# Sample's GLA products across the column groups, its state loaded earlier, more side steps in the fox gates

## The chip, the cores and the metric

One NeuronCore of a Trainium2 chip runs the whole program. The metric is the device time of one execution in microseconds, as the median of several runs. The engines are TensorE (PE, with its weight loads PEld), VectorE (DVE), ScalarE (ACT), GpSimd (POOL) and SyncE (SP, which issues most DMAs here). Each works through its own queue in order.

## The reference, cut to what matters

One layer of a hybrid decoder, in float32, for a prompt of 512 tokens and for 8 sample sequences with one new token each and 4096 cached positions in pages. Two branches run in parallel: forgetting attention (fox, 8 heads of 64) and gated linear attention (GLA, 4 heads, keys of 64, values of 128). Sigmoid gates merge them, then come an output projection and an MLP. For a sample token the GLA branch computes:

```python
b = jnp.cumsum(la, axis=1)                                   # one token: b = la
inter = jnp.einsum('blhd,bhde->blhe', qf * jnp.exp(b), S0)   # S0: (8, 4, 64, 128) state
intra = (q . k) * v                                          # with one token
S_new = exp(b)[..., None] * S0 + k (outer) v                 # returned as gla_state_sample
y = rmsnorm(inter + intra, gain) * silu(og)
```

## The kernel before, in words

Weights stream in 256 columns at a time through SP (tag raw), are split into a high part (wh, by ACT, L221) and a low part (wl, by DVE, L222), and are multiplied in three products per tile (pmm in PSUM, three buffers, two halves of 256 and 264 columns for the prompt with the samples). The main line is a list of such dense stages: fox q, k, v; gla_qk; gla_vo for values (vg) and output gates (sg); gate_f(0..3), the fox gates, each with two tanh tiles (tanh2, L1002 on, into uu) and two tiles of the fox output product; then gate_g and mix for the GLA side; then w_o and the MLP.

Two other lines of work are interleaved with it, by generators. `run(gen, nside, ndec)` advances after each dense tile the side generators by nside steps (`beside`) and the decode by an amount that follows the estimated PE time (`pump`). The decode reads the pages of keys and values of the samples (kk, kv; POOL issues these DMAs), multiplies keys on DVE (L573, L574) and values on PE (pdv). The side list holds in turn the two halves of fox for the prompt, `gla_levels` (20 steps: two for the gates, one for the diagonal, 15 for the seven levels, two that make the decayed keys kdt, with L822 to L832), `gla_sample` (five steps) and `gla_out` (four chunks of the prompt, one step each). The side work uses the px buffers of PSUM (three).

All this is program order. The framework then orders the instructions of each engine itself, by a simulated time line and with program order as priority. Buffers of a tag are slots that it hands out: a tile that is asked for (`c8()` in the code) waits until an earlier tile of the tag has had its last use. Tag c8, 8 KB per partition, has nine slots. They hold, one after another, the inputs, q and k of fox, vtok, the fox output o (two tiles, used until gate_f's last product), qk (T1, read by the levels until L827), vg, sg, then AT and bq (T2) of the levels, uu (one for gate_f(0) and (1), one for (2) and (3)), S0 of the sample, yh and yl of gla_out, and ug of gate_g. In the trace all of these are named c.

`gla_sample` first loads its state S0 (1 MB, L922). Qm holds the decayed queries spread out so that sample b's product lands in row b of its head's 32 rows. The product po adds up eight matmuls for each of four heads: head h reads rows (h%2)*64 to +64 of Qm and S0 and writes the 32 rows from h*32 of one PSUM buffer. In float32 each matmul of the code is two instructions on PE. pvo holds q.k (L939 to L942). L945 on make y, and four steps of two samples each update S0 (km, px, L974), which L977 stores.

The lines that the change touches in the main program:

```python
    for n in range(4):
        run(gate_f(n), LP, PC)
    drain("levels", "new")
```

Of the kernel before, what the change touches and what calls it, by code (L numbers as in the profile page):

```python
# [19 lines left out]
NB = 8  # L20
H = 8
GH = 4
FF = 4096
EPS = 1e-6
TS = T + NB
FP, LP, LQ = 3, 1, 1
PA, PB, PC, PD, PE_ = 1, 1.2, 0.6, 0.6, 1
LK, LV = 0, 2
TO = 1
# [20 lines left out]
def _emit(ctx, tc, I, O):  # L50
    nc = tc.nc
# [9 lines left out]
    def new(shape, tag, dt=F32, bufs=None):  # L61
        n_[0] += 1
        return sb.tile(shape, dt, tag=tag, name=f"{tag}_{n_[0]}", bufs=bufs or BUFS[tag])

    def c8(dt=F32, shape=None):
        return new(shape or [128, 4, 512], "c8", dt)
# [5 lines left out]
    def cst(shape, name, dt=F32):  # L72
        return const.tile(shape, dt, tag=name, name=name)

    def small(shape, name, bufs=2, dt=F32):
        n_[0] += 1
        return sb.tile(shape, dt, tag=name, name=f"{name}_{n_[0]}", bufs=bufs)
# [3 lines left out]
    def mm(out, lhsT, rhs, start, stop):  # L81

        clock[0] += np.prod(rhs.shape[1:]) * (4 if rhs.dtype == F32 else 1) / (4 if out.shape[0] == 32 else 1) / 2400
        PE.matmul(out=out, lhsT=lhsT, rhs=rhs, start=start, stop=stop)  # L84
# [72 lines left out]
    for lg in (4, 3, 2, 1, 0):  # L157
        a = cst([128, 32], f"lm{lg}", I32)
        b = new([128, 32], "qb", I32)
# [97 lines left out]
    def take():  # L257
        while len(ready) < 2 and plan:
            prepare()
        return ready.pop(0)  # L260
# [282 lines left out]
    gl = {}  # L543
# [164 lines left out]
    def gla_qk(w_i):  # L708
        if not w_i:
            gl["qk"] = c8()  # L710
        T1 = gl["qk"]
        w = take()[0]
        sc_ = 1.0 if w_i else 0.125
        for m in range(2):
            p0, p1 = dense_fm2(w, m, xh, xl, 8)
            S.activation(out=T1[:, 2 * w_i + m, 0:256], in_=p0[:, 0:256], func=AF.Copy, scale=sc_)
            S.activation(out=T1[:, 2 * w_i + m, 256:512], in_=p1[:, 0:256], func=AF.Copy, scale=sc_)
            S.activation(out=sq[:, 2 * w_i + m, :], in_=p1[:, 256:264], func=AF.Copy, scale=sc_)
# [6 lines left out]

    def level(sz, hp, Gt, AT, Dg):
        for e in range(2):
# [12 lines left out]
            if sz == 64:  # L740
                S.copy(out=AT[0:64, us, 64:128], in_=p[0:64, 0:256].rearrange("p (u t) -> p u t", t=64))
                continue
            p3 = p[:, 0:128].rearrange("p (u t) -> p u t", t=32)
            if sz == 32:
                for j in (0, 64):
                    S.copy(out=AT[j:j + 32, us, j + 32:j + 64], in_=p3[j:j + 32])
            elif sz == 16:
# [4 lines left out]

    def gla_levels():
        T1 = gl["qk"]
        AT = gl["AT"] = c8(shape=[128, 16, 128])
        G.memset(AT, 0.0)
        T2 = gl["bq"] = c8()

        for hp in range(2):
            p = ps("x")  # L760
            mm(p, wau[32:48, hp * 128:(hp + 1) * 128], lr[32:48, 0:512], True, True)
            x, y, a = (new([128, 512], "ts") for _ in range(3))
# [18 lines left out]
        for hp in range(2):  # L781
            pr = new([128, 512], "ts")
            V.tensor_tensor(out=pr, in0=T1[:, hp, :], in1=T1[:, 2 + hp, :], op=ALU.mult)
            for e in range(2):
# [10 lines left out]
        for u in range(len(units) + 1):  # L795
            if u < len(units):
                sz, hp = units[u]
                Et, Gt = new([128, 512], "ts"), new([128, 512], "ts")
                v4 = lambda a: a.rearrange("p (n f s) -> p n f s", f=2, s=sz)
                b4, E4, G4, q4, k4 = v4(T2[:, hp, :]), v4(Et), v4(Gt), v4(T1[:, hp, :]), v4(T1[:, 2 + hp, :])  # L800
                nb = 512 // (2 * sz)
# [6 lines left out]
            if prev is not None:  # L808
                level(*prev, AT, Dg)
            prev = (sz, hp, Gt) if u < len(units) else None  # L810
# [3 lines left out]
        for j in range(4):  # L814
            r = slice(j * 32, j * 32 + 32)
            S.copy(out=AT[r, :, r], in_=Dg[r])

        kdt = gl["kdt"] = [T2[:, hp, :].rearrange("p (c k) -> p c k", k=128) for hp in range(2)]
        for hp in range(2):
            b_, Et, kd = T2[:, hp, :], new([128, 512], "ts"), new([128, 512], "ts")  # L820
            S.activation(out=Et, in_=b_, func=AF.Exp, scale=1.0 / 16)
            V.tensor_tensor(out=T2[:, 2 + hp, :], in0=Et, in1=T1[:, hp, :], op=ALU.mult)  # L822
            bc = b_.rearrange("p (c t) -> p c t", t=128)
# [15 lines left out]
    def vo_new(is_v, n, raws):  # L839
        e, pr = sproj(hsT, raws)  # L840
        for j in range(2):
            R = slice((2 * n + j) * 32, (2 * n + j) * 32 + 32)
            mm(pr[R, 0:128], sel, e[:, j * 128:(j + 1) * 128], True, True)
        R = slice(n * 64, n * 64 + 64)
        S.copy(out=vrow[R, 0:128] if is_v else vrow[R, 128:256], in_=pr[R, 0:128])
        if is_v:
# [71 lines left out]
    ysT = cst([128, 4, 32], "ysT")  # L918

    def gla_sample():  # L920
        S0 = c8(shape=[128, 16, 128])
        nc.sync.dma_start(out=S0, in_=I["state_gla"].rearrange("o b (a e) k v -> (o e k) (b a) v", e=2))  # L922
        eas = cst([128, 2, 8], "eas")
        S.activation(out=eas, in_=las, func=AF.Exp, scale=1.0 / 16)
        Qm = new([128, 2, 256], "ts")
        G.memset(Qm, 0.0)
        V.tensor_tensor(out=Qm[:, :, 0:256:33], in0=sq[:, 0:2, :], in1=eas, op=ALU.mult)
        Qm4 = Qm.rearrange("p a (b j) -> p a b j", j=32)
        pq = small([128, 2, 32], "pq", 1)
        G.memset(pq, 0.0)  # L930
        V.tensor_tensor(out=pq[:, :, 0:8], in0=sq[:, 0:2, :], in1=sq[:, 2:4, :], op=ALU.mult)
        pvo = ps("x")
        po = ps("x")
        for h in range(GH):
            r = slice((h % 2) * 64, (h % 2) * 64 + 64)
            R = slice(h * 32, h * 32 + 32)
            for b in range(NB):
                mm(po[R, 0:128], Qm4[r, h // 2, b, :], S0[r, b * 2 + h // 2, :], b == 0, b == 7)
        for h in range(GH):  # L939
            r = slice((h % 2) * 64, (h % 2) * 64 + 64)  # L940
            R = slice(h * 32, h * 32 + 32)
            mm(pvo[R, 0:1], pq[r, h // 2, :], ones[r, 0:1], True, True)  # L942
        S.copy(out=vrow[:, 256:257], in_=pvo[:, 0:1])
        os_ = new([128, 128], "ts")
        V.scalar_tensor_tensor(out=os_, in0=vrow[:, 0:128], scalar=vrow[:, 256:257], in1=po[:, 0:128],  # L945
                               op0=ALU.mult, op1=ALU.add)
        sss = small([128, 1], "sss2")
        sumsq(os_, sss)
        rg = rsqrt(sss, 128, 1, 1.0 / 128)
        sgs = new([128, 128], "ts")  # L950
        S.activation(out=sgs, in_=vrow[:, 128:256], func=AF.Tanh, scale=0.5)
        V.scalar_tensor_tensor(out=sgs, in0=sgs, scalar=1.0, in1=vrow[:, 128:256], op0=ALU.add, op1=ALU.mult)
        V.scalar_tensor_tensor(out=os_, in0=os_, scalar=rg, in1=sgs, op0=ALU.mult, op1=ALU.mult)
        p = ps("x")
        PE.transpose(out=p[:, 0:128], in_=os_, identity=ident)
        V.tensor_scalar(out=ysT.rearrange("p a b -> p (a b)"), in0=p[:, 0:128], scalar1=ggl[:, 0:1], scalar2=None,
                        op0=ALU.mult)
        yield

        for b4 in range(4):  # L960
            km = new([8, 2, 256], "ts")
            V.tensor_tensor(out=km, in0=kst[:, None, :].to_broadcast([8, 2, 256]),
                            in1=oh8[:, 2 * b4:2 * b4 + 2, None].to_broadcast([8, 2, 256]), op=ALU.mult)
            p = ps("x")
            for b in range(2):
                for h in range(GH):
                    r = slice((h % 2) * 64, (h % 2) * 64 + 64)
                    o = (2 * b + h // 2) * 128
                    mm(p[r, o:o + 128], km[:, b, h * 64:(h + 1) * 64], vgs[:, h * 128:(h + 1) * 128], True, True)
            for b in range(2):  # L970
                for hp in range(2):
                    bi = 2 * b4 + b
                    o = (2 * b + hp) * 128
                    V.scalar_tensor_tensor(out=S0[:, bi * 2 + hp, :], in0=S0[:, bi * 2 + hp, :],  # L974
                                           scalar=eas[:, hp, bi:bi + 1], in1=p[:, o:o + 128], op0=ALU.mult, op1=ALU.add)
            yield
        nc.sync.dma_start(out=O["gla_state_sample"].rearrange("o b (a e) k v -> (o e k) (b a) v", e=2), in_=S0)  # L977

# [8 lines left out]
    def gate_f(n):  # L987
        if n % 2 == 0:
            uu.append(c8())
        w = take()[0]  # L990
        u_ = [uu[n // 2][:, 2 * (n % 2) + m, :] for m in range(2)]
        for m in range(2):
            tanh2(w, m, u_[m], sgf[:, 2 * n + m, :])
            yield
        w = take()[0]
        for m in range(2):
            p = ps("mm")
            dense_fm(p, w, m, fh, fl_, 4)
            V.scalar_tensor_tensor(out=u_[m], in0=u_[m], scalar=1.0, in1=p, op0=ALU.add, op1=ALU.mult)
            yield  # L1000
# [50 lines left out]
    def run(gen, nside=1, ndec=1):  # L1051

        for _ in gen:
            beside(nside)
            pump(ndec)
# [61 lines left out]
    side.append(("gla", gla_out()))  # L1117
    drain("fox0", "fox1")
    for n in range(4):
        run(gate_f(n), LP, PC)  # L1120
    drain("levels", "new")
    for n0 in (0, 2):
        for n in (n0, n0 + 1):
# [299 lines left out]
```

## Time and profile before

| | |
|---|---|
| median of 3 runs | 1068.72 us |
| lowest and highest | 1062.19, 1077.32 us |
| profiled execution | 1074.91 us |
| its span (first to last instruction) | 1073.2 us |
| mean granted TensorE clock | 0.964 of full |
| busy PE, DVE, ACT, POOL | 93%, 64%, 40%, 25% of the span |
| moved by DMA | 242 MB, 226 GB/s |

The times of the runs are device times without the profiler's view; all rows come from the one profiled execution. A busy PE is one that has a matmul under way, which says nothing of how full the array is.

### The profile page before, as it was taken

What the parts mean: (1) busy time and instruction counts of PE and PEld (TensorE: products, weight loads), DVE (VectorE), ACT (ScalarE), POOL (GpSimd) and SP (SyncE); (2) the same over time, 40 slices, a digit from 0 to 9 for tenths busy, and PEclk for the clock granted to TensorE, in tenths of its full rate; (3) what the DMA queues carried; (4) which work ended last, traced back from release to release, by engine and by line L of the source; (5) the groups of instructions that cost most, each with busy time, mean ns of one, the idle gap of its engine ahead of it and who ended that gap; (6) DMA issues with size and microseconds to landing.
All of it is one profiled execution on the core that took longest, in us unless ns stands there. A gap on an engine that the chain in (4) does not pass through costs nothing.

```text
span 1073.2 us, 20743 instructions
## 1 busy us (share of the span) xinstructions
PE 995.3 (93%) x8183; PEld 828.5 (77%) x8183; DVE 689.9 (64%) x1238; ACT 426.8 (40%) x1110; POOL 272.8 (25%) x256
## 2 busy tenths in 40 slices
PE   6988899999999899999894799999999799999996
PEld 5987777877967788787683677787787588888995
DVE  8568766876988858887769769667233333233356
ACT  6424444444743423333233443325423453115442
POOL 5132333244332324423434332430100000000001
PEclk9998999999999979999997899999999899999998
DMA  6736788688478637966995687894667366677222
GB/s 199 240 129 209 228 298 289 207 298 309 141 280 311 190 114 254 324 200 209 340 335 178 218 306 260 318 348 138 217 228 239 123 205 213 211 236 233 82 75 86
DMA packets 134279, 242.03 MB, mean 226 GB/s; under 512 B 11627, under 2 KB 105150, under 8 KB 125990
## 3 DMA queue, kind: packets, MB, share of 16 engines
q0 software_dynamic: 28032, 135.28, 35.7%
q1 hardware_dynamic: 106150, 105.43, 31.0%
q8 instruction: 64, 1.05, 0.4%
q14 instruction: 33, 0.27, 0.1%
HBM read 235.14 MB, written 5.47 MB: 224 GB/s over the span
## 4 chain that ended last, share of the span: by engine, by line
PE 64%; DMA 19%; issue 7%; DVE 6%; POOL 1%; ACT 1%; SPq 0%; DVEq 0%; POOLq 0%; ACTq 0%
PE pmm L84 47%; DMA kk<-in_cache_k,ixki 12%; PE px L84 10%; PE pdv L84 5%; DMA kv<-in_cache_v,ixvi 2%; DVE kk L573 2%; DMA kv<-in_w_up 1%; DVE sc L574 1%; DMA kv<-in_w_down 1%; PE pd L84 1%; DMA c<-in_state_gla 1%; DVE wl L222 1%; PE px L684 1%; POOL kk L208 0%; ACT tj L344 0%
## 5 line engine op out<-in xcount | busy, mean ns | idle before, releaser
L84 PE MATMUL pmm<-h,wh 128*128 128x256 f32 (+2 forms) x1696 | 358.7, 307 | 9.9 <-ACT h L221 4.1
L84 PEld LDWEIGHTS pmm<-h,wh 128*128 128x128 f32 x1696 | 276.7, 193 | 47.0 <-issue 19.5
L84 PE MATMUL pmm<-h,wl 128*128 128x256 f32 (+2 forms) x848 | 257.3, 306 | 0.8 <-DVE wl L222 0.8
L208 POOL DMA_INDIRECT kk<-in_cache_k,ixki x128 | 166.2, 1298 | 342.1 <-DVE sc L574 214.2
L84 PE MATMUL pmm<-wh,c 128*128 128x256 f32 x1280 | 233.1, 283 | 6.4 <-DVE c L1039 4.5
L84 PEld LDWEIGHTS pmm<-wh,c 128*128 128x128 f32 x1280 | 196.7, 189 | 28.2 <-issue 16.7
L573 DVE TENSOR_TENSOR kk<-kk,qb 128x1024 f32<-128x1024 f32 x128 | 156.5, 1223 | 92.6 <-DMA kk<-in_cache_k,ixki 90.3
L222 DVE TENSOR_TENSOR wl<-raw,wh 128x512 fp32r<-128x512 f32 x240 | 162.0, 687 | 79.4 <-PE pmm L84 55.8
L221 ACT CAST wh<-raw 128x512 fp32r<-128x512 f32 x240 | 146.4, 619 | 160.9 <-PE pmm L84 99.0
L84 PE MATMUL pmm<-wl,c 128*128 128x256 f32 x640 | 178.8, 282 | 1.6 <-DVE wl L222 1.6
L84 PEld LDWEIGHTS pmm<-h,wl 128*128 128x128 f32 x848 | 162.8, 193 | 12.6 <-issue 4.6
L574 DVE TENSOR_REDUCE sc<-kk 128x16 f32<-128x1024 f32 x128 | 154.9, 1212 | 0.7
L84 PEld LDWEIGHTS pmm<-wl,c 128*128 128x128 f32 x640 | 120.6, 189 | 10.4 <-issue 7.9
L208 POOL DMA_INDIRECT kv<-in_cache_v,ixvi x64 | 69.5, 1086 | 141.1 <-PE pdv L84 115.6
L217 POOL TENSOR_TENSOR rs<-rs,mhalf 128x1 f32<-128x1 f32 (+2 forms) x21 | 16.3, 778 | 292.7 <-DVE rs L216 291.1
L84 PE MATMUL pmm<-wh,h 128*128 128x256 f32 x384 | 77.0, 291 | 0.0
L84 PE MATMUL pdv<-kv,pt 128*32 128x512 f32 x512 | 67.8, 610 | 5.4 <-DMA kv<-in_cache_v,ixvi 5.4
L84 PEld LDWEIGHTS pmm<-wh,h 128*128 128x128 f32 x384 | 60.9, 191 | 5.0 <-issue 4.9
L84 PE MATMUL pmm<-wl,h 128*128 128x256 f32 x192 | 56.5, 295 | 1.0 <-DVE wl L222 1.0
L1338 DVE TENSOR_TENSOR c<-pmm,c 128x256 f32<-128x256 f32 x48 | 18.7, 421 | 57.1 <-PE pmm L84 56.7
L1292 DVE TENSOR_TENSOR c<-td,c 128x256 fp32r<-128x256 f32 (+1 forms) x50 | 24.8, 497 | 32.5 <-ACT td L1291 32.2
L84 PE MATMUL pmm<-c,wh 128*128 128x512 f32 x128 | 42.6, 416 | 1.6 <-DVE c L910 1.3
(335 smaller groups left out, 1099.5 us busy)
## 6 DMA issues: line engine op xcount, KB each, us to landing
raw<-in_w_in SPq DMA_DIRECT2D x80, 256.0 KB
raw<-in_w_up SPq DMA_DIRECT2D x64, 256.0 KB
raw<-in_w_down SPq DMA_DIRECT2D x64, 256.0 KB
kv<-in_w_down SPq DMA_DIRECT2D x24, 512.0 KB
kv<-in_w_up SPq DMA_DIRECT2D x18, 512.0 KB
raw<-in_w_o SPq DMA_DIRECT2D x16, 256.0 KB
kv<-in_w_o SPq DMA_DIRECT2D x8, 512.0 KB
c<-in_x_prompt SPq DMA_DIRECT2D x4, 512.0 KB
```

The source lines that it names most:

```text
L84: PE.matmul(out=out, lhsT=lhsT, rhs=rhs, start=start, stop=stop)
L208: G.indirect_dma_start(out=t, out_offset=None, in_=view, in_offset=bass.IndirectOffsetOnAxis(ap=ix[:, b, g:g + 1], axis=0))
L217: G.tensor_tensor(out=r, in0=a, in1=mhalf[:P, :n], op=ALU.pow)
L221: S.copy(out=hi, in_=raw)
L222: V.tensor_tensor(out=lo, in0=raw, in1=hi.bitcast(F32), op=ALU.subtract)
L573: V.tensor_tensor(out=K3, in0=K3, in1=qb[:, None, :].to_broadcast([128, KJ, 512]), op=ALU.mult)
L574: V.tensor_reduce(out=sc[:, g * 8 * KJ:(g + 1) * 8 * KJ], in_=K.rearrange("p (x d) -> p x d", d=64), axis=AX.X, op=ALU.add)
L684: PE.transpose(out=sp[:, kb * 128:(kb + 1) * 128], in_=P[:, kb * 128:(kb + 1) * 128], identity=ident)
L1292: V.tensor_tensor(out=l, in0=r[:, 0:n], in1=d.bitcast(F32), op=ALU.subtract)
L1338: V.tensor_tensor(out=d, in0=p, in1=d, op=ALU.add)
```

## The change

Three edits. The loop over samples goes outside the loop over heads in the products po, so that consecutive matmuls belong to four different heads. The tile S0 is asked for, and its load issued, at the first step of gla_levels, ahead of AT and bq. And gate_f runs with a constant of its own, LG = 2, in place of LP = 1, so that each of its 16 tiles advances the side list by two steps.

```diff
-FP, LP, LQ = 3, 1, 1
+FP, LG, LP, LQ = 3, 2, 1, 1
...
     def gla_levels():
         T1 = gl["qk"]
+        S0 = gl["S0"] = c8(shape=[128, 16, 128])
+        nc.sync.dma_start(out=S0, in_=I["state_gla"].rearrange("o b (a e) k v -> (o e k) (b a) v", e=2))
         AT = gl["AT"] = c8(shape=[128, 16, 128])
         G.memset(AT, 0.0)
         T2 = gl["bq"] = c8()
...
     def gla_sample():
-        S0 = c8(shape=[128, 16, 128])
-        nc.sync.dma_start(out=S0, in_=I["state_gla"].rearrange("o b (a e) k v -> (o e k) (b a) v", e=2))
+        S0 = gl["S0"]
...
-        for h in range(GH):
-            r = slice((h % 2) * 64, (h % 2) * 64 + 64)
-            R = slice(h * 32, h * 32 + 32)
-            for b in range(NB):
+        for b in range(NB):
+            for h in range(GH):
+                r = slice((h % 2) * 64, (h % 2) * 64 + 64)
+                R = slice(h * 32, h * 32 + 32)
                 mm(po[R, 0:128], Qm4[r, h // 2, b, :], S0[r, b * 2 + h // 2, :], b == 0, b == 7)
...
     for n in range(4):
-        run(gate_f(n), LP, PC)
+        run(gate_f(n), LG, PC)
     drain("levels", "new")
```

## Rows read from the trace of the kernel before

**Rows 1.** The page: busy time, share of the span and instructions.

```profile
PE 995.3 (93%) x8183; PEld 828.5 (77%) x8183; DVE 689.9 (64%) x1238; ACT 426.8 (40%) x1110; POOL 272.8 (25%) x256
```

**Rows 2.** Windows: length, PE PEld DVE ACT POOL busy, granted clock, DMA, GB/s.

```profile
285.00:360.00 75.00, 71.95 (x1139) 58.34 (x1140) 67.62 (x137) 36.30 (x103) 26.16 (x22) 0.95 0.69 238
360.00:374.00 14.00, 9.94 (x89) 8.70 (x77) 10.95 (x19) 4.30 (x9) 5.25 (x2) 1.00 0.79 254
374.00:385.00 11.00, 11.00 (x74) 9.16 (x73) 4.14 (x6) 2.13 (x6) 2.50 (x3) 0.52 0.40 123
```

**Rows 3.** Chain of work that ended last: start, us, what.

```profile
364.38 9.28 DMA c<-in_state_gla
373.79 10.82 PE px L84 x71
```

**Rows 4.** Timeline of PE: start, us, operation, count, idle before and its releaser.

```profile
373.79 10.12 PE L84 MATMUL px<-c,ts 64*32 64x128 f32 x61 [4.06 <-DMA c<-in_state_gla]
```

**Rows 5.** Windows of one us, PE alone: length, busy, granted clock, DMA.

```profile
387.00:388.00 1.00, 1.00 (x6) 0.50 0.00 0
388.00:389.00 1.00, 1.00 (x10) 0.99 0.00 0
```

**Rows 6.** Timeline of PE: decode values, a level, last products of gla_out.

```profile
415.53 1.92 PE L84 MATMUL pdv<-kv,pt 128*32 128x512 f32 x16
...
359.22 1.05 PE L84 MATMUL px<-ts 64*32 64x32 f32 x96
...
444.17 1.20 PE L84 MATMUL px<-c,c 128*128 128x128 f32 x12
```

**Rows 7.** Line 756, the memset of AT: min/median/max ns, first and last start.

```profile
L756 POOL MEMSET c<- x1: 1818/1818/1818, 241.1 to 241.1; 128x2048 f32 x1
```

**Rows 8.** Timeline of PE and ACT: fox's last product with v, uu0's first write.

```profile
281.75 1.00 PE L84 MATMUL px<-c,ts 128*128 128x64 f32 x8
...
284.98 0.38 ACT L1005 ACTIVATE c<-pmm 128x256 f32<-128x256 f32 x1
```

**Rows 9.** Timeline of DVE and SP: qk's last reader, the load of S0.

```profile
363.61 0.69 DVE L827 TENSOR_TENSOR ts<-ts,c 128x512 f32<-128x512 f32 x1
...
364.38 0.86 SPq L922 DMA_DIRECT2D c<-in_state_gla  x1
```

**Rows 10.** Timeline of PE, SP and ACT around gate_g(0)'s first tanh.

```profile
408.95 0.58 PE L84 MATMUL pmm<-h,wh 128*128 128x256 f32 x1
...
411.36 0.38 SPq L977 DMA_DIRECT2D out_gla_state_sample<-c  x1
...
424.24 0.68 ACT L909 ACTIVATE c<-px,vcol 128x512 fp32r<-128x512 f32 x1
...
425.06 0.39 ACT L1005 ACTIVATE c<-pmm 128x256 f32<-128x256 f32 x1
```

**Rows 11.** Timeline of ACT: gate_f(2)'s first and third tanh.

```profile
347.79 0.39 ACT L1005 ACTIVATE c<-pmm 128x256 f32<-128x256 f32 x1 [0.16 <-PE pmm L84]
...
356.67 0.36 ACT L1005 ACTIVATE c<-pmm 128x256 f32<-128x256 f32 x1
```

**Rows 12.** Groups of DVE by line, 356 to 446 us: busy us, mean ns, idle.

```profile
L573 DVE TENSOR_TENSOR kk<-kk,qb 128x1024 f32<-128x1024 f32 x14 | 17.1, 1223 | 3.9 <-DMA kk<-in_cache_k,ixki 3.8
...
L974 DVE SCALAR_TENSOR_TENSOR c<-c,eas,px 128x128 f32<-128x128 f32 x16 | 4.5, 352 | 0.0
...
L927 DVE TENSOR_TENSOR ts<-sq,eas 128x16 f32<-128x16 f32 x1 | 0.2, 197 | 0.0
```

**Rows 13.** Windows of PE by tile: two of px, one of pdv.

```profile
356.00:374.00 18.00, 2.29 (x106) 1.00 0.67 211
...
385.00:445.40 60.40, 17.00 (x153) 0.95 0.70 232
...
385.00:445.40 60.40, 7.54 (x55) 0.95 0.70 232
```

**Rows 14.** Timeline of DVE: the levels' diagonal, their last write of Dg.

```profile
371.50 0.72 DVE L812 COPY_PREDICATED Dg<-lmd,aself 128x512 f32<-128x512 int32 x1
```

## The prediction

> **What bounds the kernel now.** I read the page first [rows 1]: TensorE (PE) is busy 93% of the span, VectorE (DVE) 64%, but that is a mean over stages. So I cut the stretch that the change touches into windows [rows 2]. From 285 to 360 us PE is busy 71.95 of 75 us and DVE 67.62: both are close to full. From 360 to 374 PE loses 4 us, and from 374 to 385 it is busy throughout at a granted clock of 0.52, while DVE does 4.1 us of work in 11. The chain of work that ended last [rows 3] names the two causes: the load of the sample's GLA state, 9.28 us on the path, and 10.82 us of PE on px tiles. The timeline of PE [rows 4] says that PE stood still for 4.06 us until the state had landed, and then issued 61 of the 64 matmuls of sample's products in 10.12 us. The clock fell behind that stop and stayed at half (1.2 GHz) until 388 [rows 5]. So the stage pays for one late transfer three times: the stop, slow products, and dense work at half clock behind them.
>
> **Part 1, the four heads side by side.** The same 64 matmul instructions remain; only their order changes, so that neighbours write different 32-column groups. What that is worth is shown by two rows [rows 6]. The value products of the decode, 128x32 tiles with four neighbours in four column groups, take 1.92 us for 16 instructions of 512 columns, 0.030 us per 128 columns; 64 of them would be 1.9 us. The levels' 64x32 tiles, also four column groups, take 1.05 us for 96 instructions of 32 columns, which is 0.044 us per 128 columns, or 2.8 us. Those rows include the last result's way out. I take 2.2 us at full clock, nearer to the first row, whose instructions are long ones like these. The change is 10.82 - 2.2 = 8.6 us, if the clock stays up.
>
> One thing differs from both rows: here neighbours also lie in different row halves (heads 0 and 2 in rows 0 to 63, 1 and 3 in rows 64 to 127) and share one PSUM bank. If that puts them in file again, the price is the present one at full clock: 10.12/61 = 0.166 us each at half clock [rows 4], 0.083 at full, 5.3 us for 64. The Trainium skill, TensorEngine Tiling (Array Packing), section Restrictions and Gotchas, says just this: different row tiles cannot use one PSUM bank at the same time. No row of this trace decides it; by that rule the products take 5.3 us rather than 2.2.
>
> **Part 2, the state loaded at the head of the levels.** The stop of 4.06 us goes, and with it the fall of the clock; the dense work from 384.6 to 388 at half clock gets back half of 3.4 us, 1.7 us. The DMA itself (1 MB) moves ahead in SP's queue. What it costs is a slot of c8. There are nine slots. At the head of the levels o (two tiles), qk, vg and sg live, beside what is left of the second fox half. Now S0 takes the slot that AT takes before: AT's memset ran at 241.1 us [rows 7], so the load can start about there, more than 100 us ahead of its use. On SP the loads of weights queue behind it; as its slot is free they wait only for its issue, and PE's later work is many loads away. I cost it at nothing; without that cover it is the transfer itself, at most its 9.28 us [rows 3]. AT, bq and uu0 then take the slots of fox's q, k and v tiles. v is last read by PE at 281.75 + 1.00 and uu0 first written at 284.98 [rows 8], so that hand-over fits with 2.2 us to spare; AT and bq get theirs earlier. POOL's memset of AT moves later, past some page loads: 1.8 us on POOL, hidden while AT isn't read.
>
> The nine are then full: o twice, qk, vg, sg, S0, AT, bq, uu0. Before, one was free, uu1 took it, and S0 waited on SP for qk: its load was issued at 364.38, when the last reader of qk, L827, ended (363.61 + 0.69) [rows 9]. So the wait for qk doesn't vanish; it moves to the next that asks.
>
> **Part 3, two side steps per tile.** The side generators give 12 steps of the levels to the gla_vo tiles. Before, the 16 tiles of gate_f give levels 13 to 20, five steps of sample, and three of gla_out. Now gate_f(0) gives levels 13 to 20, gate_f(1) the whole of sample and three steps of gla_out, and gate_f(2) the fourth. All their instructions go along: the POOL memsets, the output DMA of the state on SP, DVE, ACT. They are ahead of decode steps that they stood behind, each 2.43 us of DVE. In itself this only shifts priority: in the trace the side work runs behind its place in the program anyway.
>
> But it also changes the order of the slots. gla_out asks for yh and yl, and now does so ahead of uu1, the target of gate_f(2)'s tanh. Do slots go out in the order of the program, or to whoever writes first? gate_g(0) answers [rows 10]. Its first accumulator had its last wh product at 408.95 + 0.58; two slots (o's) had fallen free when fox's last product was done. ACT's tanh of it, L1005, ran only at 425.06, behind the first write of yh at 424.24, with ACT idle for much of the time between. yh and yl had been asked for earlier and held o's two slots unwritten; the tanh's tile had to take S0's, whose store was issued at 411.36. So I take it that slots go in program order.
>
> Then after the change yh gets qk's slot, yl that of S0 (after the store), and uu1 the third, which is AT's, bq's or vg's: free when the last chunk of gla_out has been multiplied. Until then gate_f(2)'s tanh can't be written. Its first tile was written at 347.79 and the third accumulator read at 356.67 [rows 11]; PSUM has three for dense work. So dense work stops at about 356 us and PE has only side and decode work until gla_out's last products.
>
> How long? DVE carries that chain. In 356 to 446 us the side's own DVE work is 24 us, 17 groups from L974 (4.5 us) to L927 (0.2 us) [rows 12]; about 2 us of it (L824, L822) will lie ahead of the stop. The decode gets a step per 6.4 us (14 in 90 us), five in such a stretch, at 2.43 us. So 22 + 5 x 2.43 = 34 us. PE's work in it: px tiles, 2.29 + 17.0 us and 2.2 for the new products, is 21.5; the decode's products, 7.54 us in 60.4, give 4.2 in 34 [rows 13]. That is 26, all of which has to be done somewhere. The net cost of the stop is 34 - 26 = 8 us. Small matmuls with waits between them may also run at half clock: none of it, or as much as the 10 us that those products would lose if most ran so; I take 2 us.
>
> **Sum.** -4.06 - 8.6 - 1.7 = -14.4; +8 + 2 = +10; net -4.4 us. The profiled execution took 1074.91 us (span 1073.2 and 1.7 around it), so 1070.5 in its terms. It lies 6 us above the median of the three runs, 1068.72, inside their 15 us. Against the median the forecast is 1064 us. What follows the stage is shifted, not shortened: I count nothing for it.
>
> **Rivals.**
> (A) Slots go to the first writer. Then uu1 takes qk's as the levels end, dense work stops for about 1 us, and the whole -14.4 is kept: -13, 1055 us. The late tanh speaks against it [rows 10]; that L827's end started the load at once [rows 9] fits both.
> (B) Slower: the stop lasts as long as that chain takes today. From L812 at 371.50 [rows 14] to the last products of gla_out, 444.17 + 1.20 [rows 6], are 73.9 us; less 2.3 of the wait and 8.6 of the block that is 63, and 2 from 356 to the levels' end make 65. PE has 21.5 + 7.5 = 29 us of work for it: 36 us lost, net +21, 1090 us. It decides against the change once the stop is over 26 + 14 = 40 us. For it: the rsqrt steps on POOL stand behind page loads, and each chunk needs PE, ACT, POOL and DVE in turn. Against it: today each of these steps also queues behind dense tiles on PE.
> (C) Row halves in one bank go in file: 5.3 for 2.2, so -1.3 us, 1067.
> (D) The change doesn't do what it says: PE's stop has a second cause as late. At 369.7 all three dense accumulators were held too, DVE standing for a page of keys. If pages set the pace here, the gain is taken back: 1069.
>
> **How the numbers follow.** The forecast 0.50, A 0.22, B 0.14, C 0.07, D 0.07. The forecast's own range, from 2.8 us for the products and 10 us for the clock to none, and 6 us either way on the stop's length, is 1056 to 1079. For eight in ten I go to 1051 (A with the spread of the runs) and 1083, which leaves out most of B. Two per cent, about what a measurement of this kernel can tell from no change, is 1047 and 1090: faster 0.06, same 0.85, slower 0.09 (some more than half of B).
>
> **What would show it.** Right: the load issued near 241, no PE wait on it; 64 px matmuls of 64x32 in 1.9 to 2.8 us at full clock; a stretch of some 34 us without pmm matmuls in gate_f(2), ended by gla_out's last products, with gate_f(2)'s third and later tanh behind it; gate_g free of px work. Wrong: dense tiles going on through the sample step (A), the products at 0.08 us each (C), or a stop above 40 us (B). The forecast itself fails if the planner puts the instructions into quite another order on the engines, so that decode or weights come late elsewhere.

## The result and the profile after

The changed kernel is slower: 1114.36 us median of six runs against 1070.75 us of six runs of the kernel before, ratio 1.037 (1.031 to 1.043). The ratio is that of the fast runs alone: two of the changed kernel's six, the profiled one among them, and one of the six before count as slow, and a fast run of almost the same program (the first try below) shows the same stop of dense work. The forecast was 1064, the range ended at 1083. The profiled execution of the changed kernel took 1117.56 us, 3 us over its median. (Its code lines stand one or two lower than before: L1005 to L1007 are L1007 to L1009, L909 is L911, L974 is L976.)

The page first. PE's line is the one that answers to [rows 1]:

```profile
PE 1004.7 (90%) x8183; PEld 828.9 (74%) x8183; DVE 693.1 (62%) x1238; ACT 427.6 (38%) x1110; POOL 271.7 (24%) x256
```

The same instructions, but PE is busy 9.4 us longer and idle 1115.9 - 1004.7 = 111.2 us, against 1073.2 - 995.3 = 77.9 before. So 33.3 us of the 42.7 us of longer span are idle PE and 9.4 are slower work.

Where? The timeline of PE (start, us, operation, count, what ended the idle time before) shows the last dense product (pmm) and the next one:

```profile
362.50 0.28 PE L84 MATMUL pmm<-h,wl 128*128 128x256 f32 x1
...
373.58 3.50 PE L84 MATMUL px<-c,ts 64*32 64x128 f32 x64
...
441.80 0.61 PE L84 MATMUL px<-c,c 128*128 128x128 f32 x4
...
442.67 0.66 PE L84 MATMUL px<-c,c 128*64 128x128 f32 x8
444.25 0.51 PE L84 MATMUL pmm<-h,wh 128*128 128x264 f32 x2
```

Dense work stops from 362.78 to 444.25, 81.5 us, and resumes right after gla_out's last products: the place and the end that the prediction named, at more than twice its length. The longest stretch without pmm in this part of the trace of before is 14.8 us. Windows over exactly these 81.47 us, PE PEld DVE ACT POOL busy, granted clock, DMA, GB/s, first of the kernel after:

```profile
362.78:444.25 81.47, 44.42 (x497) 30.57 (x497) 63.04 (x114) 16.90 (x64) 32.73 (x30) 0.69 0.62 204
```

and of the kernel before:

```profile
362.78:444.25 81.47, 77.30 (x580) 65.08 (x580) 60.13 (x116) 25.32 (x82) 28.44 (x25) 0.90 0.68 225
```

PE idles 37.05 us of it after and 4.17 before: 32.9 us, practically the whole 33.3 of the program. What PE does in the stop it does at a mean granted clock of 0.69.

ACT's timeline shows who was waiting: the tanh of gate_f(2) stands behind two of yh's writes and is released by gla_out's products on px (compare [rows 11], where it ran at 347.79):

```profile
417.65 0.68 ACT L911 ACTIVATE c<-px,vcol 128x512 fp32r<-128x512 f32 x1
430.22 0.68 ACT L911 ACTIVATE c<-px,vcol 128x512 fp32r<-128x512 f32 x1
442.45 0.39 ACT L1007 ACTIVATE c<-pmm 128x256 f32<-128x256 f32 x1 [11.54 <-PE px L84]
...
443.56 0.72 ACT L911 ACTIVATE c<-px,vcol 128x512 fp32r<-128x512 f32 x1
```

The tanh runs 0.04 us after the last chunk's 128x128 products (441.80 + 0.61), the last to read AT. vg, and bq with the decayed keys in it, are read once more at 442.67. So its slot was AT's, the first of the three that the prediction named.

What fills the 81 us? The groups of DVE by line in the stop (count | busy us, mean ns | idle before and its releasers), which answer to [rows 12]:

```profile
L573 DVE TENSOR_TENSOR kk<-kk,qb 128x1024 f32<-128x1024 f32 x16 | 19.6, 1222 | 16.9 <-DMA kk<-in_cache_k,ixki 16.9
L574 DVE TENSOR_REDUCE sc<-kk 128x16 f32<-128x1024 f32 x16 | 19.4, 1212 | 0.2
L976 DVE SCALAR_TENSOR_TENSOR c<-c,eas,px 128x128 f32<-128x128 f32 x16 | 4.4, 340 | 0.6 <-PE px L84 0.6
```

Sixteen decode steps, 39.0 us busy, and 16.9 us in which DVE stood at the head of its queue for a page of keys. DVE's other work in the stop is 63.04 - 39.0 = 24.0 us. The three add up to 79.9 of 81.5 us, so DVE had next to no idle time but for pages. That is how its queue was filled; how long the chain of GLA's chunks would be without decode these rows don't say.

The state's load answers to [rows 9]; the view of line 756 (ns, first and last start) puts it 136 us earlier, and no PE wait names it:

```profile
L756 SPq DMA_DIRECT2D c<-in_state_gla x1: 861/861/861, 228.5 to 228.5; - x1
```

### The profile page after: what moved, and what is told of

The parts are those of the page before. It is cut to its first block, busy times and chain, and to the rows that moved or that the text cites. A ratio compares the mean times of both kernels' runs of the same rounds, so it can differ in the third digit from the quotient of the medians.

```text
span 1115.9 us, 20764 instructions
## 1 busy us (share of the span) xinstructions
PE 1004.7 (90%) x8183; PEld 828.9 (74%) x8183; DVE 693.1 (62%) x1238; ACT 427.6 (38%) x1110; POOL 271.7 (24%) x256
## 3 DMA queue, kind: packets, MB, share of 16 engines
q8 instruction: 64, 1.05, 0.4%
## 4 chain that ended last, share of the span: by engine, by line
PE 49%; DMA 26%; DVE 10%; issue 10%; POOL 2%; ACT 1%; another core or an unknown queue 1%; SPq 1%; POOLq 0%; DVEq 0%; ACTq 0%
PE pmm L84 37%; DMA kk<-in_cache_k,ixki 18%; PE px L84 7%; PE pdv L84 4%; DVE sc L574 3%; DMA kv<-in_cache_v,ixvi 3%; DVE kk L573 3%; DMA kv<-in_w_down 2%; DMA raw<-in_w_in 1%; DVE wl L222 1%; DMA raw<-in_w_fox_out 1%; POOL kk L208 1%; PE pd L84 1%; DMA kv<-in_w_o 1%
## 5 line engine op out<-in xcount | busy, mean ns | idle before, releaser
L84 PE MATMUL pmm<-wh,c 128*128 128x256 f32 x1280 | 230.7, 281 | 0.4 <-DVE c L1041 0.4
L84 PE MATMUL pdv<-kv,pt 128*32 128x512 f32 x512 | 77.7, 651 | 23.7 <-DMA kv<-in_cache_v,ixvi 19.2
L1291 ACT ACTIVATE td<-pmm 128x256 f32<-128x256 f32 (+1 forms) x50 | 22.1, 442 | 67.6 <-PE pmm L84 64.5
```

The source lines that it names most:

```text
L1291: S.activation(out=r[:, 0:n], in_=p[:, 0:n], func=AF.Relu)
```

## The experiments

The theory after the result: gate_f(2) waits for a c8 slot that comes free with gla_out's last products, and the wait is long since DVE runs decode steps, and waits for their pages, between the steps of that chain. The rivals: the products or the early load cost the time (not the slots); the two side steps are slow in themselves; the chain is long by its own hand-offs, with or without decode. Parts 1, 2 and 3 are the three edits of the diff. Ratios are to the kernel before on the same chip.

**Each part alone, and 1 with 2.** The edits are the hunks of the change.

Part 1 alone. 

> Part 1 alone: the loop over samples outside that over heads, everything else as before. Theory (the slots of c8 made the loss): this part is good; S0 still arrives late, so PE's wait of some 4 us on the state stays and the clock still falls, but the 64 products take 3.5 us at half clock instead of 10.1; ratio to before 0.990 to 0.997 (-7 us). Rival (neighbours in different row halves of one bank go in file): the products take 10 us as before and the ratio is 1.00.

Part 2 alone. 

> Part 2 alone: the state asked for and loaded at the head of the levels, one side step per tile, products in the old order. Theory: uu1 now waits for qk, that is for the levels' end, a stop of dense work of 1 to 10 us in gate_f(2) instead of the 4 us wait on the state; the products take 5 to 7 us at full clock; ratio 0.985 to 1.00. Rival (the early tile is what costs 40 us, whatever the steps): ratio 1.03 and a stop of dense work of 50 us or more.

Part 3 alone. 

> Part 3 alone: two side steps per tile of gate_f, state asked for in sample, old products. Theory: yh and yl are asked for ahead of uu1 here too, so gate_f(2)'s tanh again waits for gla_out's end: a stop of dense work of 70 to 90 us, ratio 1.03 to 1.05 by this part alone. Rival (only the early S0 fills the nine slots): uu1 finds a slot, no stop above 15 us, ratio 0.98 to 1.00.

Parts 1 and 2. 

> Parts 1 and 2 without part 3. Theory: uu1 waits for qk alone (stop of 1 to 10 us), no wait on the state, the 64 products in 2 to 3.5 us; ratio 0.982 to 0.995 (-5 to -19 us), the best of the four. Rival (the early tile costs): ratio 1.02 or more.

| kernel | ratio | interval | longest stretch without pmm near the sample step |
|---|---|---|---|
| 1 | 0.9948 | 0.9913 to 0.9982 | 367.88 to 373.97, 6.1 us |
| 2 | 0.9996 | 0.9964 to 1.0027 | 360.83 to 379.25, 18.4 us |
| 3 | 1.0206 | 1.0159 to 1.0252 | 349.57 to 416.87, 67.3 us |
| 1 and 2 | 0.9992 | 0.9969 to 1.0014 | 356.60 to 368.00, 11.4 us |

The stop comes with part 3 and stands there without the others; there too gate_f(2)'s tanh (416.06) runs behind two of yh's writes. Part 1 gains, part 2 shows no gain, and the two together none either (0.9992 for part 1's 0.9948, intervals that overlap). Not all went as expected: part 1 came out in its range, with a wait of 3.69 us for the state and then 64 products in 2.42 us instead of 3.5, as the clock fell only among them (0.78 granted). Part 3 stayed under its 70 to 90 us and 1.03 to 1.05. The stretches of part 2 and of 1 and 2 are over their 10 us, and the two parts together missed their 0.982 to 0.995. Part 3 alone costs 2.1% and the whole change 3.7%, so some 1.6% come only when parts 1 and 2 are added to part 3, with a stop that is 14 us longer. Part 3 with one of the others was not run, so which of them does it is open.

Why part 2 alone is worth nothing shows in its timeline of PE, where the products start without any wait for the state and are as slow as ever:

```profile
367.94 10.68 PE L84 MATMUL px<-c,ts 64*32 64x128 f32 x61
```

They came right after PE's waits for the levels' end on DVE. Dense work had stopped at 360.83 because gate_f(2)'s first tanh now waits for qk's slot, as the expectation said; ACT runs it when L829, qk's last reader, has ended on DVE (366.08 + 0.69):

```profile
366.81 0.39 ACT L1006 ACTIVATE c<-pmm 128x256 f32<-128x256 f32 x1 [2.93 <-DVE ts L829]
```

So the wait for qk moved from the state to the fox gates' tile, and PE idled and its clock fell (0.64 granted from 364 to 366, 0.50 behind that) without the late load.

**Who gets a slot, first try.** The whole change, but the fox gates' second tile is asked for at gate_f(0):

```diff
-        if n % 2 == 0:
-            uu.append(c8())
+        if n == 0:
+            uu.extend((c8(), c8()))
```

> The whole change, but both uu tiles are asked for at gate_f(0), so that uu1 stands ahead of yh and yl in the order of the slots; nothing else is edited. Theory (slots in program order made the stop): uu1 gets qk's slot at the levels' end, dense work stops for 1 to 12 us in gate_f(2) instead of 82, and the ratio to before is 0.98 to 1.00. Rival (two side steps per tile push splits and decode back on VectorE, whatever the slots): the time stays near the changed kernel's, ratio 1.03.

Measured: 1.0282 (1.0238 to 1.0326), the stop still 82.6 us, gate_f(2)'s tanh at 433.36. That expectation fell: when a tile is asked for does not decide.

**One slot more.** The whole change with `c8=10` (two small tiles of decode's end moved to another tag to make room).

> The whole change with ten slots of c8 in place of nine (two small tiles of the decode's end share another tag to make room). Theory: yh takes the tenth, yl that of qk, uu1 that of S0, after the store of the state: the stop ends with the store (40 us after its start in the changed kernel) instead of with gla_out's end, 40 to 50 us long in place of 82, and the ratio is 1.00 to 1.02. Rival (priority of the side steps): no difference from the changed kernel, 1.03 to 1.04.

Measured: 1.0251 (1.0209 to 1.0293), the stop 57.8 us: shorter and faster than the changed kernel, but outside both expected ranges. On SP the state's store is issued at 396.96:

```profile
396.96 0.38 SPq L979 DMA_DIRECT2D out_gla_state_sample<-c  x1
```

and ACT writes gate_f(2)'s tanh behind the first chunk, not the last:

```profile
409.96 0.68 ACT L911 ACTIVATE c<-px,vcol 128x512 fp32r<-128x512 f32 x1
410.78 0.39 ACT L1007 ACTIVATE c<-pmm 128x256 f32<-128x256 f32 x1
```

This is the picture of [rows 10], one tile further on: with one slot more, the fox gates' tile moves up from the slot freed by the last chunk to, as I read it, the one freed by the store of S0. No row names what released this tanh; it runs 13.8 us after the store's issue, where gate_g's in [rows 10] ran 13.7 after it.

**The first writer.** Ten slots as before, and the second tile is also written at gate_f(0):

```diff
+        if n == 0:
+            uu.extend((c8(), c8()))
+            G.memset(uu[1][:, 0, 0:8], 0.0)
```

> The whole change with ten c8 slots, and the fox gates' second tile (uu1) asked for and written (eight columns set to zero on GpSimd) at the start of gate_f(0), ahead of gla_out's first step. If c8 slots go to whoever writes first in the program, uu1 now has its slot before yh and yl, so gate_f(2)'s tanh no longer waits for the last chunk of gla_out: no stretch without dense products over 15 us between 340 and 450 us, gate_f(2)'s tanh by 385 us, ratio to the kernel before 0.985 to 1.00. If the two side steps per tile are slow by themselves (side work in place of decode, whoever holds the slots), the ratio stays at 1.02 to 1.03 and a stretch of 40 us or more is left.

Measured: 1.0102 (1.0042 to 1.0163). The stop is gone: ACT's timeline has gate_f(2)'s first tanh at

```profile
340.85 0.39 ACT L1008 ACTIVATE c<-pmm 128x256 f32<-128x256 f32 x1 [9.38 <-PE pmm L84]
```

70 us ahead of the same kernel without the early write, and the longest stretch without pmm is 11.5 us (442.17 to 453.64), at another place. So the place of the first write decides and not that of the request, and this order made the stop. It is the order in the program, not in time: in the changed kernel qk's last reader ended at 371.73 + 0.68, with gate_f(2)'s accumulators full since 362.78, and still yh, first written at 417.65, went ahead of the tanh. The ratio missed its 0.985 to 1.00: 1.0% stays with no stop to blame.

**Decode out of the way.** First the whole change without decode steps given out between gate_f's tiles, `run(gate_f(n), LG, 0)`.

> The whole change, with no decode steps given out during gate_f (they follow in gate_g and later; all work is done). It asks what made the stop 82 us rather than 34. Theory (the chain shares VectorE and GpSimd in order with decode steps that wait for pages): fewer page steps lie in the stop, each chunk of gla_out takes under 9 us instead of 12.5, and the stop is 40 to 60 us. Rival (the chain's own round trips set its pace): 12 to 13 us per chunk and a stop of 75 us or more. The total time isn't the point: the decode ends later.

Measured: 1.0322 (1.0258 to 1.0386), the stop 74.1 us, between the two ranges, and still 14 decode steps in it. As I read it the steps that were given out earlier lag behind their place, and the planner draws later ones forward. The edit didn't take away what it was to take away, so it can't decide between the two. One thing it does show: DVE waits 6.0 us for pages in this stop, 10.9 less than in the changed kernel, and has two decode steps fewer (4.9 us), but the stop is only 7.4 us shorter. DVE now also waits 5.7 us for rsqrt and for products of PE, where it had waited about 1 us. So a wait for a page covers hand-offs of the chain in part, and the three terms above don't come off one for one. Then a hold that the planner can't get around: decode's query row is written again only after the first two mix tiles (zero times a value from a late tile is added to it), and until then no decode steps are given out.

```diff
-        owed[0] += (clock[0] - seen[0]) * rate / TAU
+        owed[0] += (clock[0] - seen[0]) * rate / TAU * hold[0]
...
+        if not hold[0]:
+            hold[0] = 1.0
+            V.scalar_tensor_tensor(out=q8, in0=ug[0][0:8, 3, 504:512], scalar=0.0, in1=q8, op0=ALU.mult, op1=ALU.add)
+            nc.sync.dma_start(out=qd[:, 0:8], in_=q8)
```

> The whole change with nine slots, but the decode's score steps cannot start before the first two mix tiles are through (its query row is written again then, with a zero multiple of a late tile added), so nothing of decode but its first two page loads lies beside the GLA chain. All decode comes later, so the whole time is not to be compared (1150 to 1400 us); what is read is the stop of dense products ahead of gate_f(2). If the stop is long because the chain shares VectorE, GpSimd and ScalarE in order with decode that waits for pages, it shrinks from 81.5 to 15 to 35 us, near the 22 us of side work that the prediction counted for the chain. If the chain is long by its own hand-offs between engines, it stays over 50 us.

Measured: 1315.02 us in one run, all of decode being late; the longest stretch without pmm at this place is 12.8 us (325.74 to 338.57), below even the 15 to 35 us that were expected. The order of the slots is the same: gate_f(2)'s tanh, L1011 here, still comes behind two of yh's writes (L915).

```profile
321.06 0.69 ACT L915 ACTIVATE c<-px,vcol 128x512 fp32r<-128x512 f32 x1 [5.37 <-PE px L913]
329.17 0.68 ACT L915 ACTIVATE c<-px,vcol 128x512 fp32r<-128x512 f32 x1
337.24 0.38 ACT L1011 ACTIVATE c<-pmm 128x256 f32<-128x256 f32 x1 [6.74 <-PE px L84]
```

The two kernels can be compared from the start of sample's products to the pmm with which gate_f(2) goes on. In the kernel after, all of it without dense work:

```profile
373.58:444.25 70.67, 39.43 (x297) 26.79 (x297) 52.27 (x96) 14.42 (x60) 29.38 (x27) 0.69 0.68 227
```

and without decode, with dense work beside it until 325.74:

```profile
295.35:338.57 43.22, 38.93 (x338) 34.25 (x338) 21.79 (x62) 12.94 (x48) 4.46 (x5) 0.84 0.22 62
```

Without decode the stretch is 27.5 us shorter than the 70.7. DVE works 21.79 us instead of 52.27, and POOL 4.46 instead of 29.38. The 43.2 us that are left are twice DVE's work in them, so the rival of the hand-offs has a share too: DVE's groups there show it idle for PE's products and for POOL's rsqrt. PE is busy for 38.93 of the 43.22 us, so dense tiles ahead of the chain's products are part of that; no run has the chain without either.

```profile
L909 DVE SCALAR_TENSOR_TENSOR ts<-px,rs,c 128x128 f32<-128x128 f32 x12 | 3.4, 344 | 3.6 <-POOL rs L217 3.6
...
L899 DVE SCALAR_TENSOR_TENSOR Dg<-Dg,eb,px 64x128 f32<-64x128 f32 x8 | 2.8, 347 | 3.0 <-PE px L84 2.8
```

But here the chain starts ahead of the need for its slot and lies mostly beside dense work; only 12.8 us of it are bare. (Without decode the levels and the chain also run some 78 us earlier in the program, so this kernel shows both at once, a shorter chain and a better cover, and not how much each of them took off the 81.5 us.)

**A better version.** Three searches with ten slots: parts 1 and 2; part 1 alone; part 1 with the early write of the fox gates' second tile.

> The products side by side and the early load of S0, one side step per tile as in the kernel before, ten c8 slots. If the early load alone gave back what the products gain because S0 holds a slot from the levels on, the tenth slot frees it: longest stretch without dense products under 8 us, ratio 0.985 to 0.995, the best so far. If the early load is worth nothing and the loss lay elsewhere, the ratio is that of the two parts with nine slots, 0.997 to 1.001.

> Products side by side alone, with ten c8 slots: a search for a version that beats both kernels. If a slot is still short with S0 loaded late, the ratio falls below the 0.9948 of the products alone, to 0.985 to 0.993; if no slot is short there any more, it stays at 0.993 to 0.998.

> The same with the fox gates' second tile written first at the start of gate_f(0). If slots go to the first writer, gate_f(2)'s tanh and yh change places in the queue for a slot: gate_f(2) earlier, gla_out's first chunk later or equal, ratio 0.985 to 0.998. If the order of slots is of no weight with ten, the result is that of the run before within 0.5%.

| with ten slots | ratio | interval |
|---|---|---|
| 1 and 2 | 1.0014 | 0.9982 to 1.0047 |
| 1 | 0.9892 | 0.9864 to 0.9921 |
| 1, early write | 0.993 | 0.9903 to 0.9956 |

Part 1 with ten slots, 1058.8 us, beats both kernels. The kernel before with ten slots was not run, so what the slot is worth without part 1 is not known. With it the load of S0 goes out at 344.2 us without having been moved in the program (362.8 in part 1 alone with nine slots), no PE wait names it, and PE is busy for all of 362 to 385 us at full clock. That is the range expected if a slot is still short with S0 loaded late. The last two rows can't be told apart; of the order expected in the last, gate_f(2)'s tanh did come earlier (344.26 for 346.99), but yh's first write came earlier as well (407.67 for 414.42) where it was to come later or at the same time. The first search fell: its longest stretch without pmm was 6.7 us at this place, under the 8 expected, but the tenth slot did not make the early load pay. Against part 1 alone with ten slots the early load costs 1.2%. The slot of AT isn't the reason, as I first thought from nine slots, where AT's memset moved from 241.1 to 268.5 us: with ten it runs at 238.20, and the levels' last products still come at 368.60, against 361.05 without the early load. What delays the levels is open in the main. One part is the clock: from 340 to 360 us, among the levels' products, it is 0.68 with the early load and 1.00 without it, in one execution of each. One small cost of the early load is in this trace: PE waits 2.0 us for weights at 232 and 236 us, behind S0's load at 226.5; part 1 alone with ten slots has no such wait, nor have parts 1 and 2 with nine.

In this best version the products, at full clock, are

```profile
369.82 1.95 PE L84 MATMUL px<-c,ts 64*32 64x128 f32 x64
```

## Why the prediction was wrong

The mechanism of the forecast happened: yh and yl came ahead of uu1, gate_f(2) waited until the last chunk was multiplied, dense work stopped. The step that failed is "How long?", and in it two things: the term "five in such a stretch, at 2.43 us", and the waits, which it put at nothing by adding up DVE's busy time alone. I took the number of decode steps from a length that it was itself to determine, 34 us at one step per 6.4 us. But the steps stand in DVE's queue in a fixed order between those of the chain; the chain moves on only as decode does.

| term of the stop | forecast | measured |
|---|---|---|
| other work on DVE | 22 us, side work alone | 24.0 us, 3.1 of it other work of decode |
| decode steps on DVE | 5 x 2.43 = 12 us | 16 x 2.44 = 39.0 us |
| DVE waiting for pages | 0 | 16.9 us |
| length | 34 us | 79.9 of 81.5 us |

The table says what filled DVE's queue, not what each row would save: with all of decode gone the compared stretch shrank by 27.5 us, and what was left, 43.2 us for 21.8 of DVE's work, was still longer than the forecast's sum. So waits on other engines, too, were missing from it; how many of them would be left where dense work stands still and decode is gone no run shows.

So the stop went over the 40 us from which the prediction let rival B decide, and over B's own 65. B's price was low for the same reason: it took the chain's length beside dense work, where DVE waited for pages 3.9 us in 90 [rows 12]. With dense work gone decode went from 13 steps in this window to 16, each 5.1 us apart, and had to wait for the pages.

- **Net cost of the stop, +8 and +2.** The idle of PE grew by 33.3 us, and 4.06 of the old idle were gone: 37.4 us for the forecast's 8. PE's busy time grew by 9.4 us although the products fell from 10.12 + 0.84 to 3.50, 7.5 less: 16.9 us for the forecast's 2, at a granted clock of 0.69 in the stop. The two terms are 44 us too small; -4.4 + 44 is +40, and the rest to the measured +42.7 of span are the products (7.5 gained for 8.6) and the clock's 1.7.
- **Products, -8.6.** Right: 64 in 1.95 us at full clock with ten slots, where I took 2.2. In the kernel after they fall into the stop and take 3.50 us. Rival C is out: by its row of 0.083 us each they would take 5.3. The rule that stood behind it (the Trainium skill, TensorEngine Tiling (Array Packing), Restrictions and Gotchas) differs from these rows: neighbours in different row halves and one bank did not go in file. Here they write different partitions of that bank; no run has them on the same ones.
- **Wait for the state, -4.06, and the clock behind it, -1.7.** The load went to 228.5, and no PE wait names it. But with nine slots the fox gates' tile then waits for qk in its place, and the clock falls anyway (part 2 alone: 10.68 us for 61 products, ratio 0.9996). So the early load by itself did not bring these terms; rival D said as much, for a page of keys instead of the levels, and rival A's 1 us for such a wait was too low (stretches of 18.4 and 11.4 us without pmm). With ten slots PE is busy for all of 362 to 385 us at full clock, with the load early or late, but only with it late did the time fall.
- **The early load at no cost.** Wrong: 0.4% with nine slots (parts 1 and 2 against 1, intervals that overlap), 1.2% with ten.
- **Slots in program order.** Right against rival A, but it is the order of the first write and not, as I put it, of the request.
- **Follow-on.** I counted nothing for what comes after the stage. Part 1 alone has its last tanh of gate_f(3) 11 us earlier than before, and its profiled span is 9.6 us shorter; over all runs it gains 0.5%, about 5.6 us. How much is given back later can't be told within the spread of the runs.

Open: with ten slots and no stop the whole change stands at 1.0102, where part 1 alone stands at 0.9892. Of these 2.1% the early load takes 1.2 (1.0014 for 0.9892) and the two side steps with the early write 0.9 (1.0102 for 1.0014, intervals that just overlap). No run tells by which wait either does it; the 2.0 us for weights and the low clock from 340 to 360 us are what the one pair of traces shows of the early load's share.

## What to carry to other kernels

When a change can make an engine wait for a chain, count the chain in the queue of the engine that carries it: every instruction that stands between its steps, those of other work too, with their own waits, and the hand-offs to other engines, which busy time leaves out. A rate (steps per microsecond) from a stretch without the stop says nothing of that; a count taken from a length that it is to determine is no estimate. And when tiles of a tag change places, list who writes first, and what each next writer's slot waits for; one slot more may be worth as much as the edit that was made (0.9892 for 0.9948 with part 1 here, intervals that just overlap).

## What the runs showed of the hardware

Sixty-four 64x32 matmul instructions of 128 columns in float32, neighbours in four column groups, from alternating row halves and into different partitions of one PSUM bank, take 1.95 us at full clock, 0.030 us each, as the decode's 128x32 ones in [rows 6]; in file they were 0.166 at half clock. Near half clock (granted 0.56 and 0.53) they take 3.34 and 3.50 us. In the stop PE was busy 44.42 of 81.47 us, in short pieces with waits between them, and had a mean granted clock of 0.69; so the clock was low for work that the chain needed.
